# The forget gate's low-rank product on the unsplit residual, with the norm's column factors in its weights

## The chip, the cores and the metric

The kernel runs on one core of one Trainium2 chip. The metric is the time of one execution on the device, in microseconds (us). The engines are named as in the profile: PE multiplies matrices, PEld is its weight loads, DVE and ACT work elementwise, POOL does a few odd jobs and issues some DMAs, SP issues the other DMAs.

## The reference

One layer of a streaming encoder: 512 positions, model width 1024, all in float32.

```python
h = h + 0.5 * swiglu(rmsnorm(h, ffn1_norm), ffn1_w_in, ffn1_w_out)
z = rmsnorm(h, mix_norm) @ w_in
conv_a, conv_gt, q, k, v, r, g_lr = split(z)       # g_lr: 16 columns
y_conv = conv_module(conv_a, conv_gt, ...)          # GLU, causal depthwise conv of width 31, LayerNorm, silu
log_a = log_sigmoid(g_lr @ gate_w_up + gate_b) / 16 # forget gate, through rank 16
y_gla = gla(q, k, v, r, log_a)                      # chunked gated linear attention
h = h + concat([y_conv, y_gla]) @ w_out
h = h + 0.5 * swiglu(rmsnorm(h, ffn2_norm), ...)
h = h + sigmoid(rmsnorm(h, ple_norm) @ ple_w_gate) * (p @ ple_w_proj)
out = rmsnorm(h, final_norm)
```

`rmsnorm(h, g)` is `h * rsqrt(mean(h*h) + eps) * g`: a factor for each row (position) and a factor `g` for each column. The product that this case is about is `g_lr`, 1024 to 16.

## The kernel before, in words

Activations lie transposed: a tile holds 128 columns of the model (partitions) by 512 positions, so the residual is eight tiles `hT[0..7]`. Float32 products are made from fast ones: each operand is split into a high and a low part, and three products (high by high, high by low, low by high) are added in PSUM (`mm3`). For the mixer the residual is first multiplied by `mix_norm`'s column factors and then split; these eight pairs are `hg`. The row factor is not in them: it is multiplied in behind each product, by DVE, with the tile `bc` (`rsb` in the code), which holds the row factors spread over all partitions.

The engines' orders are the order of the code: `Ordered` chains the instructions of PE, DVE and ACT in the order in which they are written. POOL's order is left to the scheduler. Matmuls and nearly all else are recorded at L46, in that helper; what is told apart is told by tiles.

The place of the change is the start of the mixer, behind the first feed-forward part. PE makes, one after the other, with `zblock` (24 matmuls of 128x512: eight column tiles, three products each), the convolution's gate and value columns in blocks of 128: `pb0`, `pa0`, `pb1`, `pa1`, and later two more pairs. Two short steps are put between the matmuls of a `zblock`, through its argument `mid`: in `pa0` the column sums of squares (`colsum`), from which DVE and POOL make the row factors (`rsqrt_mean`: DVE `ms`, POOL `rs`, four small DVE instructions); in `pb1` the four transposes that spread them (`spread`), behind which ACT copies the result to `bc`. From then on DVE multiplies `bc` into `pb0` (tile `g`, then ACT's sigmoid, tile `s`) and `pa0` (`u`), makes the gated value (`glu_out`), and fills its time with the convolution's taps (`taps(n)`: n instructions of 482 to 511 positions each, tile `cv`).

The low-rank product stood behind `pa1`: its weights `gw` (128 x 8 x 32, both 16 columns and padding) were multiplied with `hg` as plain float32, in four 32-column strips of the array that sum every fourth column tile, once for the high and once for the low parts. That is 16 matmuls of 32x512; a plain float32 matmul stands in the trace as two records. DVE multiplied the result with `bc` (tile `glr`, named `glu` in the trace, since it shares a buffer with it), and PE's next product but one, with `gwu`, read it. `gw` is loaded by SP (L1036).

PSUM is eight banks; `bank()` hands them out in turn. At the end of the mixer PE waits in places on DVE and ACT: DVE finishes the taps, `y` times `r` is made for the attention's output, PE transposes it, and the LayerNorm of the convolution runs through DVE, ACT and PE.

Of the kernel before, what the change touches and what calls it, by code (L numbers as in the profile page):

```python
# [8 lines left out]
F32 = mybir.dt.float32  # L9
# [3 lines left out]
ALU = mybir.AluOpType  # L13
PSUM = bass.MemoryType.PSUM

P = 128
SEQ = 512
D = 1024
DC = D // P
# [8 lines left out]
TB = SEQ // P  # L28
RANK = 16
# [33 lines left out]
def block_kernel(ctx: ExitStack, tc: tile.TileContext, a: dict, out: bass.AP):  # L63
    nc = tc.nc
    pe, dve, act, pool = (Ordered(tc, e) for e in (nc.tensor, nc.vector, nc.scalar, nc.gpsimd))
# [15 lines left out]
    def nm(s):  # L81
        uid[0] += 1
        return f"{s}_{uid[0]}"
# [6 lines left out]
    def bt2(dt=F32R, s="a"):  # L90
        t = big.tile([P, 2, SEQ], dt, tag="A", bufs=NA, name=nm(s))
        hi, lo = t[:, 0], t[:, 1]
        whole_of[id(hi)] = hi, t
        return hi, lo

    def bt(dt=F32, s="a"):
        if dt not in other:
            t, other[dt] = bt2(dt, s)
            return t
        return other.pop(dt)  # L100
# [4 lines left out]
    def tmp(s, w=SEQ, dt=F32, bufs=2):  # L105
        return tp.tile([P, w], dt, tag=s, bufs=bufs, name=nm(s))
# [14 lines left out]
    def psum(pool_, n, shape, tag="mm"):  # L121
        return pool_.tile(shape, F32, tag=tag, bufs=n, name=nm("pd" if len(shape) == 3 else "ps"))

    def singles():
        return region("fixed", "spare" if mode[0] == 0 else stack[1][0] if len(stack) > 1 else "double", "singles")

    def bank():
        if mode[0] == 0:
            turn_no[0] += 1
            at = turn_no[0] % 7  # L130
            if at in (3, 4):
                return fixed()
            if at in (5, 6):
                return spare()
        return psum(singles(), 3, [P, SEQ])

    def fixed():
        return psum(region("fixed"), 2, [P, SEQ])

    def spare():  # L140
        return psum(region("fixed", "spare"), 2, [P, SEQ])
# [10 lines left out]
    def aux():  # L152
        if mode[0] == 2:
            return fixed()
        return psum(singles(), 1, [P, SEQ], "aux")
# [14 lines left out]
    col = cp.tile([P, ncol + 4 * WIDTH], F32, name="col")  # L170
    nc.scalar.dma_start(out=col, in_=a["columns"])
    cw = col[:, ncol:ncol + 4 * WIDTH]
    first_of, at = {}, 0
# [1 line left out]
        first_of[name] = at  # L175
        at += n

    def vec(name, c):
        at = first_of[name] + c
        return col[:, at:at + 1]  # L180

    warm = cp.tile([P, 1], F32, name="warm")
    act.copy(warm, ones)
# [39 lines left out]
    def high(r3):  # L223

        nk, nc_ = r3.shape[1], r3.shape[2]
        hi = wp.tile([P, 1024], F32R, tag="wh", bufs=6, name=nm("wh"))
        lo = wp.tile([P, 1024], F32R, tag="wl", bufs=6, name=nm("wl"))
        h3 = hi[:, :nk * nc_].rearrange("p (k c) -> p k c", k=nk)
        l3 = lo[:, :nk * nc_].rearrange("p (k c) -> p k c", k=nk)
        act.copy(h3, r3)  # L230
        return h3, l3, r3
# [17 lines left out]
    def mm3(ps, wh, wl, xh, xl, first, last):  # L249
        pe.matmul(ps, wh, xh, start=first, stop=False)  # L250
        pe.matmul(ps, wh, xl, start=False, stop=False)
        pe.matmul(ps, wl, xh, start=False, stop=last)
# [15 lines left out]
    def rows_of(w, k):  # L268

        part, kk = (w[k // 4], k % 4) if isinstance(w, list) else (w, k)  # L270
        return part[0][:, kk, :], part[1][:, kk, :]

    def zblock(w, x, mid={}):

        ps = bank()
        for k in range(DC):
            if k in mid:
                mid[k]()
            wh, wl = rows_of(w, k)
            mm3(ps, wh, wl, *x[k], k == 0, k == DC - 1)  # L280
        return ps

    def rsqrt_mean(ss, n, w, bufs=3, between=None):

        ms = tmp("ms", 16)[:, :w]
        dve.tensor_scalar(ms, ss, 1.0 / n, EPS, ALU.mult, ALU.add)
        r = tmp("rs0", 16)[:, :w]
        pool.tensor_tensor(out=r, in0=ms, in1=negh[:, :w], op=ALU.pow)
        if between is not None:
            between()  # L290
        t = tmp("rs1", 16)[:, :w]
        dve.tensor_tensor(out=t, in0=r, in1=r, op=ALU.mult)
        dve.tensor_tensor(out=t, in0=t, in1=ms, op=ALU.mult)
        dve.tensor_scalar(t, t, -0.5, 1.5, ALU.mult, ALU.add)
        rs = tmp(f"rs{bufs}", 16, bufs=bufs)[:, :w]
        dve.tensor_tensor(out=rs, in0=r, in1=t, op=ALU.mult)
        return rs

    def spread(col, copy=True):

        ps = aux()
        for j in range(TB):
            pe.transpose(ps[:, j * P:(j + 1) * P], col[:, j:j + 1].to_broadcast([P, P]), ident)
        if not copy:
            return ps
        bc = tmp("bc", bufs=1)
        act.copy(bc, ps)
        return bc

    def colsum(srcs):  # L310

        ps = aux()
        n = 0
        for s in srcs:
            for j in range(TB):
                pe.matmul(ps[:, n * TB + j:n * TB + j + 1], s[:, j * P:(j + 1) * P], ones,
                          start=True, stop=True)
            n += 1
        if n == 1:
            return ps[:, 0:TB]  # L320
        t = tmp("cs", 16)[:, :TB]
        dve.tensor_reduce(out=t, in_=ps[:, :n * TB].rearrange("p (n j) -> p j n", j=TB),
                          axis=mybir.AxisListType.X, op=ALU.add)
        return t
# [172 lines left out]
    hT = [big.tile([P, SEQ], F32, tag="H", bufs=DC, name=nm("h")) for _ in range(DC)]  # L497
    hg = []
# [49 lines left out]
    norm, mid = Norm(), []  # L548
# [400 lines left out]
    def sums_hooks(x, names, at):  # L949

        h = {}
        for name, key in zip(names, at):
# [14 lines left out]
    hg, norm = ffn(ffn1_in, a["ffn1_w_out"][0], xb, "mix_norm", {0: Left(ffn1_in, 0), 1: w1, 2: w2},  # L967
                   (ps0[:2], ps0[2:]), lambda: spread(mid[0]), hooks, (1,), FAR, CASTS, ADDS)
# [15 lines left out]
    def conv_steps(c):  # L984
        y, g, tap = acc[c], glu[c], cw[:, c * WIDTH:(c + 1) * WIDTH]
        dve.tensor_scalar(y, g, tap[:, PAD:WIDTH], vec("conv_b", c), ALU.mult, ALU.add)
        yield
        for w in range(PAD):
            late = PAD - w
            dve.scalar_tensor_tensor(out=y[:, late:], in0=g[:, 0:SEQ - late], scalar=tap[:, w:w + 1],  # L990
                                     in1=y[:, late:], op0=ALU.mult, op1=ALU.add)
            yield
# [22 lines left out]
    def glu_value(ps):  # L1015
        a1 = tmp("u1")
        dve.tensor_tensor(out=a1, in0=ps, in1=rsb, op=ALU.mult)
        return a1

    def glu_out(a1, sg):  # L1020
        g = bt(s="glu")
        dve.tensor_tensor(out=g, in0=a1, in1=sg, op=ALU.mult)
        glu.append(g)
        conv.append(conv_steps(len(glu) - 1))


    wb, wa = w_ahead
# [5 lines left out]
    mid = []  # L1033
    pb0 = zblock(wb[0], hg)
    gw = bt(s="gw")[:, 0:2 * DC * RANK].rearrange("p (k c) -> p k c", k=DC)
    nc.sync.dma_start(out=gw, in_=a["gate_down"])  # L1036
    w2a.append(high(raw_a[1]))
    raw_q = pair(C_Q)
    low(w2a[0])
    pa0 = zblock(wa[0], hg, {1: lambda: mid.append(rsqrt_mean(colsum([norm.acc]), D, TB))})  # L1040
    low(w2a[1])
    pb1 = zblock(wb[1], hg, {1: lambda: mid.append(spread(mid[0]))})
    rs, rsb = mid
    rs2 = tmp("rs2", 16, bufs=1)[:, :TB]
    dve.tensor_tensor(out=rs2, in0=rs, in1=rs, op=ALU.mult)
    raw_k = pair(C_K)
    sg = glu_gate(pb0)
    v = glu_value(pa0)
    glu_out(v, sg)
    wq = [added(high(raw_q[0]))]  # L1050
    taps(3)
# [4 lines left out]

    ps = bank()
    for k0 in range(0, DC, 4):  # L1060
        for i in range(2):
            for j in range(4):
                pe.matmul(ps[2 * RANK * j:2 * RANK * (j + 1)], gw[:, k0 + j, :], hg[k0 + j][i].bitcast(F32),
                          start=(k0 == i == 0), stop=(k0 + i == 5), skip_group_check=True)
    glr = bt(s="glr")
    taps(1)
    dve.tensor_tensor(out=glr, in0=ps, in1=rsb, op=ALU.mult)
    wq.append(added(high(raw_q[1])))


# [7 lines left out]
    for j in range(2):  # L1078
        ps = bank()
# [79 lines left out]
    k0 = zblock(wk[0], hg)  # L1159
# [115 lines left out]
    for t in range(TB):  # L1275
        ps = tokblock(wv, t, {5: lambda: chunk_sums(range(6)),
                             8: lambda: wr.append(high(raw_r[2])),
                             14: lambda: wr.append(high(raw_r[3]))} if t == 3 else {})
# [57 lines left out]
    for t in range(TB):  # L1336
        if t == 0:
            taps(3)
            ps = tokblock(wr, t, {5: lambda: chunk_sums([6]), 12: lambda: outputs(0)})
            chain(range(4, 7))  # L1340
            oload(4)
        elif t == 1:
            ps = tokblock(wr, t, {2: lambda: outputs(1)})
# [7 lines left out]
                                     in1=rs.unsqueeze(2).to_broadcast([P, TB, 4]), op0=ALU.mult, op1=ALU.mult)  # L1351
        else:
            ps = tokblock(wr, t)
# [90 lines left out]
    norm = Norm()  # L1444
# [25 lines left out]
    for k in range(4):  # L1470
        for n in range(3):
            w, ps = half[n]
# [22 lines left out]
    hg = nhg  # L1495
# [17 lines left out]
    mid = []  # L1513
# [97 lines left out]
    hg, norm = ffn(ffn2_in, a["ffn2_w_out"][0], xb, "ple_norm", wf, ((g0, u0), (g1_, u1_)), mid[1], hooks, (), {("m5", 1): 4, ("m6", 2): 3, ("m1", 3): 3, ("m2", 3): 3}, {("m6", 2): 4, ("m1", 3): 4})  # L1611
# [299 lines left out]
```

## Time and profile before

| | us |
|---|---|
| median of 3 runs | 930.98 (929.45 to 931.45) |
| the profiled execution | 929.6 |
| its span, first to last instruction | 927.9 |
| PE busy | 918.3 (99%) |
| DVE busy | 823.0 (89%) |
| ACT busy | 507.8 (55%) |
| granted TensorE clock, mean | 0.998 |

The profiled execution took 1.7 us more than its span, and 1.4 us less than the median. Start times are counted from the first instruction. PE's rows overlap: a matmul's record is longer than the distance to the next one's start, so that the cost of a matmul in a row of many is read from starts, not from durations.

### The profile page before, as it was taken

The page shows a single profiled execution, that of the slowest core. Times are in us where ns is not written, and L with a number is a line of the kernel's source. Part 1 is how long each engine was busy: PE and PEld are TensorE (multiplying, and loading weights), DVE is VectorE, ACT ScalarE, POOL GpSimd, SP SyncE. Part 2 cuts the span into 40 slices and gives each one's busy share as a digit, 9 for nine tenths or more (in the row PEclk, how much of TensorE's full clock was granted, in tenths as well). Part 3 has the DMA queues.
Part 4 walks back from the last instruction along what each step waited for, and adds up shares of the span by engine and source line. Part 5 has one row for each costly group of instructions (what it writes and reads, how often), then busy time and mean ns, then how long its engine had stood idle before and what let it go on. Part 6 is the DMA issues. An engine that isn't in the chain of part 4 may idle for free.

```text
span 927.9 us, 12878 instructions
## 1 busy us (share of the span) xinstructions
PE 918.3 (99%) x4982; PEld 782.4 (84%) x4982; DVE 823.0 (89%) x1098; ACT 507.8 (55%) x740; POOL 58.3 (6%) x73
## 2 busy tenths in 40 slices
PE   9999999999999999999999999999999999999996
PEld 8898888888888888788877889888888888888885
DVE  6699989999999876999986789899999999997896
ACT  7664355445444574463564875355445444456883
POOL 0120000000000111001120020000000000000120
PEclk9999999999999999999999999999999999999999
DMA  9433334224322693356552563334224322348463
GB/s 325 116 91 120 108 115 128 88 80 133 118 91 65 155 260 93 74 130 138 137 137 75 153 141 109 114 114 125 87 85 130 120 91 78 110 136 244 91 113 115
DMA packets 104175, 114.44 MB, mean 123 GB/s; under 512 B 3889, under 2 KB 90289, under 8 KB 104113
## 3 DMA queue, kind: packets, MB, share of 16 engines
q1 hardware_dynamic: 97664, 94.65, 32.8%
q0 software_dynamic: 6304, 18.88, 11.2%
q8 instruction: 39, 0.64, 0.3%
q14 instruction: 24, 0.19, 0.1%
q10 hardware_dynamic: 144, 0.09, 0.0%
HBM read 93.67 MB, written 2.10 MB: 103 GB/s over the span
## 4 chain that ended last, share of the span: by engine, by line
PE 99%; DVE 1%; issue 0%; ACT 0%; POOLq 0%; DVEq 0%
PE ps L46 59%; PE pd L46 40%; DVE u L46 0%; DVE rs L46 0%; ACT yc L46 0%; DVE y L46 0%; DVE g L46 0%; DVE s L46 0%; DVE yc L46 0%; POOLq L1907 0%; DVE ms L46 0%; DVE zeros L46 0%; DVE sse L46 0%; DVEq L46 0%; POOLq L46 0%
## 5 line engine op out<-in xcount | busy, mean ns | idle before, releaser
L46 DVE TENSOR_TENSOR wl<-wr,wh 128x1024 fp32r<-128x1024 f32 (+2 forms) x161 | 188.3, 1180 | 16.3 <-ACT wh L46 16.1
L46 ACT CAST wh<-wr 128x1024 fp32r<-128x1024 f32 (+2 forms) x178 | 176.2, 1021 | 20.7 <-PE ps L46 6.4
L46 PE MATMUL pd<-hg,wh 128*128 128x512 f32 x576 | 150.0, 391 | 0.0
L46 PE MATMUL ps<-act,wh 128*128 128x512 f32 x448 | 138.3, 390 | 0.0
L46 PEld LDWEIGHTS pd<-hg,wh 128*128 128x128 f32 x576 | 105.9, 188 | 21.0 <-DVE u L46 0.4
L46 PE MATMUL ps<-hg,wh 128*128 128x512 f32 (+1 forms) x448 | 117.3, 346 | 0.0
L46 PE MATMUL pd<-t,wh 128*128 128x512 f32 x392 | 98.2, 392 | 0.0
L46 PEld LDWEIGHTS ps<-act,wh 128*128 128x128 f32 x448 | 83.1, 188 | 16.5
L46 ACT ACTIVATE s<-g 128x512 f32<-128x512 f32 x48 | 30.4, 633 | 117.9 <-DVE g L46 117.9
L46 ACT COPY sq<-pd 128x1024 f32<-128x1024 f32 x45 | 45.7, 1016 | 87.3 <-PE pd L46 52.9
L46 PEld LDWEIGHTS ps<-hg,wh 128*128 128x128 f32 x448 | 78.0, 190 | 11.3 <-issue 1.3
L46 PE MATMUL ps<-act,wl 128*128 128x512 f32 x224 | 87.1, 389 | 0.0
L46 PE MATMUL pd<-hg,wl 128*128 128x256 f32 (+1 forms) x544 | 83.9, 289 | 0.0
L46 PEld LDWEIGHTS pd<-hg,wl 128*128 128x128 f32 x544 | 75.9, 190 | 6.3
L46 PEld LDWEIGHTS pd<-t,wh 128*128 128x128 f32 x392 | 70.5, 189 | 12.6
L46 PE MATMUL ps<-hg,wl 128*128 128x512 f32 (+1 forms) x224 | 77.1, 344 | 0.0
L46 ACT CAST wh<-sm 128x1024 fp32r<-128x1024 f32 x42 | 44.0, 1051 | 54.7 <-DVE sm L46 50.5
L46 PEld LDWEIGHTS pd<-t,wl 128*128 128x128 f32 x392 | 53.5, 190 | 3.8
L46 DVE TENSOR_TENSOR wl<-sm,wh 128x1024 fp32r<-128x1024 f32 x42 | 50.9, 1219 | 4.9 <-ACT wh L46 4.9
L46 DVE TENSOR_TENSOR sq<-pd,sq 128x1024 f32<-128x1024 f32 x45 | 54.8, 1218 | 0.4 <-PE pd L46 0.4
L46 PE MATMUL ps<-wh,hg 128*128 128x512 f32 x176 | 54.8, 392 | 0.0
L46 PE MATMUL pd<-t,wl 128*128 128x256 f32 x392 | 54.7, 282 | 0.0
(307 smaller groups left out, 1636.9 us busy)
## 6 DMA issues: line engine op xcount, KB each, us to landing
wr<-in_ffn_w_in SPq DMA_DIRECT2D x84, 512.0 KB, 3.7
wr<-in_ffn_w_out SPq DMA_DIRECT2D x32, 512.0 KB, 3.5
wr<-in_w_in SPq DMA_DIRECT2D x20, 512.0 KB, 5.1
wl<-wr POOLq DMA_DIRECT2D x18, 512.0 KB, 5.3
wr<-in_ffn_w_out SPq DMA_DIRECT2D x16, 384.0 KB, 3.1
wr<-in_w_out SPq DMA_DIRECT2D x8, 512.0 KB, 4.0
wq<-in_ple_w_gate SPq DMA_DIRECT2D x8, 512.0 KB, 3.8
wl<-wq POOLq DMA_DIRECT2D x8, 512.0 KB, 4.9
```

The lines of the kernel that those rows point to most:

```text
L46: inst = call(*args, **kwargs)
```

## The change

The low-rank product is made once, from the unsplit residual `hT`, instead of twice from the parts of `hg`. The column factors of `mix_norm`, which `hg` contains and `hT` does not, are multiplied into the weights `gw` by one DVE instruction (`gains`), put into `rsqrt_mean` between POOL's instruction and the four small ones of DVE. The eight matmuls stand directly behind the transposes of `spread`, inside `pb1`; the product with `bc` stands behind `pa0`'s, ahead of the first gated value.

```diff
@@ -175,9 +175,9 @@
         first_of[name] = at
         at += n
 
-    def vec(name, c):
+    def vec(name, c, n=1):
         at = first_of[name] + c
-        return col[:, at:at + 1]
+        return col[:, at:at + n]
 
     warm = cp.tile([P, 1], F32, name="warm")
     act.copy(warm, ones)
@@ -1034,18 +1034,35 @@
     pb0 = zblock(wb[0], hg)
     gw = bt(s="gw")[:, 0:2 * DC * RANK].rearrange("p (k c) -> p k c", k=DC)
     nc.sync.dma_start(out=gw, in_=a["gate_down"])
+    low_rank = []
+
+    def gains():
+        dve.tensor_tensor(out=gw, in0=gw, in1=vec("mix_norm", 0, DC).unsqueeze(2).to_broadcast([P, DC, 2 * RANK]),
+                          op=ALU.mult)
+
+    def spread_and_low_rank():
+        mid.append(spread(mid[0]))
+        ps = bank()
+        for k0 in range(0, DC, 4):
+            for j in range(4):
+                pe.matmul(ps[2 * RANK * j:2 * RANK * (j + 1)], gw[:, k0 + j, :], hT[k0 + j],
+                          start=(k0 == 0), stop=(k0 == 4), skip_group_check=True)
+        low_rank.append(ps)
+
     w2a.append(high(raw_a[1]))
     raw_q = pair(C_Q)
     low(w2a[0])
-    pa0 = zblock(wa[0], hg, {1: lambda: mid.append(rsqrt_mean(colsum([norm.acc]), D, TB))})
+    pa0 = zblock(wa[0], hg, {1: lambda: mid.append(rsqrt_mean(colsum([norm.acc]), D, TB, between=gains))})
     low(w2a[1])
-    pb1 = zblock(wb[1], hg, {1: lambda: mid.append(spread(mid[0]))})
+    pb1 = zblock(wb[1], hg, {1: spread_and_low_rank})
     rs, rsb = mid
     rs2 = tmp("rs2", 16, bufs=1)[:, :TB]
     dve.tensor_tensor(out=rs2, in0=rs, in1=rs, op=ALU.mult)
     raw_k = pair(C_K)
     sg = glu_gate(pb0)
     v = glu_value(pa0)
+    glr = bt(s="glr")
+    dve.tensor_tensor(out=glr, in0=low_rank[0], in1=rsb, op=ALU.mult)
     glu_out(v, sg)
     wq = [added(high(raw_q[0]))]
     taps(3)
@@ -1056,15 +1073,7 @@
 
 
 
-    ps = bank()
-    for k0 in range(0, DC, 4):
-        for i in range(2):
-            for j in range(4):
-                pe.matmul(ps[2 * RANK * j:2 * RANK * (j + 1)], gw[:, k0 + j, :], hg[k0 + j][i].bitcast(F32),
-                          start=(k0 == i == 0), stop=(k0 + i == 5), skip_group_check=True)
-    glr = bt(s="glr")
     taps(1)
-    dve.tensor_tensor(out=glr, in0=ps, in1=rsb, op=ALU.mult)
     wq.append(added(high(raw_q[1])))
 
 
```

On PE, at `pb1` (`ps_3309` before, `ps_3310` in the change) and the four transposes of the row factors (`ident`), `gw` are the low-rank weights, `hg` the split and `h` the unsplit residual. Before:

```order
L46 MATMUL ps_3309<-hg_3066,wa_2943 128x512 x3
L46 MATMUL ps_3313<-ident,rs_580_3285 128x128 x4
L46 MATMUL ps_3309<-hg_3078,wa_2943 128x512 x3
...
L46 MATMUL ps_3366<-hg_3192,wa_3046 128x512 x3
L46 MATMUL ps_3402<-hg_3066,gw_3258 32x512
...
L46 MATMUL ps_3402<-hg_3192,gw_3258 32x512
L46 MATMUL ps_3426<-hg_3066,wh_3214 128x512 x2
```

In the change, at the same place:

```order
L46 MATMUL ps_3310<-hg_3066,wa_2943 128x512 x3
L46 MATMUL ps_3314<-ident,rs_580_3286 128x128 x4
L46 MATMUL ps_3321<-h_104,gw_3258 32x512
...
L46 MATMUL ps_3321<-h_111,gw_3258 32x512
L46 MATMUL ps_3310<-hg_3078,wa_2943 128x512 x3
...
L46 MATMUL ps_3378<-hg_3192,wa_3046 128x512 x3
L46 MATMUL ps_3419<-hg_3066,wh_3214 128x512 x2
```

The 16 matmuls between `pa1` and the next block are gone, and eight stand between the transposes and the rest of `pb1`.

On DVE, from the row factors (`ms`, `rs`) to the first block's taps (`cv`). Before:

```order
L46 TENSOR_SCALAR ms_3277<-ps_3272 128x4
L46 TENSOR_TENSOR rs_579_3281<-rs_578_3279 128x4
...
L46 TENSOR_TENSOR g_587_3347<-ps_3233,bc_3318 128x512
L46 TENSOR_TENSOR u_589_3351<-ps_3268,bc_3318 128x512
L46 TENSOR_TENSOR gw_3258<-u_589_3351,s_3349 128x512
...
L46 TENSOR_TENSOR g_592_3362<-ps_3309,bc_3318 128x512
...
L46 TENSOR_TENSOR glu_3400<-ps_3402,bc_3318 128x512
L46 TENSOR_SCALAR cv_3203<-glu_3400,col 128x512
```

In the change:

```order
L46 TENSOR_SCALAR ms_3277<-ps_3272 128x4
L46 TENSOR_TENSOR gw_3258<-gw_3258,col 128x256
L46 TENSOR_TENSOR rs_579_3282<-rs_578_3279 128x4
...
L46 TENSOR_TENSOR g_588_3357<-ps_3233,bc_3319 128x512
L46 TENSOR_TENSOR u_590_3361<-ps_3268,bc_3319 128x512
L46 TENSOR_TENSOR gw_3258<-ps_3321,bc_3319 128x512
L46 TENSOR_TENSOR glu_3364<-u_590_3361,s_3359 128x512
...
L46 TENSOR_TENSOR g_594_3374<-ps_3310,bc_3319 128x512
```

The weights' factor is new between `ms` and `rs`; the low-rank result's product (named `glu` before and `gw` now, for the buffer it shares) stands two rows behind `g` instead of at the end of the second block's taps. POOL's two instructions that set the tile `keep` come ahead of two DMAs instead of behind them.

## The prediction

> **What bounds the kernel now.** First the page: busy shares and the chain that ended last.
>
> ```profile
> PE 918.3 (99%) x4982; PEld 782.4 (84%) x4982; DVE 823.0 (89%) x1098; ACT 507.8 (55%) x740; POOL 58.3 (6%) x73
> PE 99%; DVE 1%; issue 0%; ACT 0%; POOLq 0%; DVEq 0%
> ```
>
> PE is both the busiest engine and nearly the whole chain. A time taken off PE should therefore come off the end, as long as nobody else sets PE's starts. So next PE's waits (in total, times, longest), and the stretches of the mixer (PE, PEld, DVE, ACT, POOL busy, then clock, DMA share and GB/s).
>
> ```profile
> PE ps L46 <- DVE zeros L46: 1.1, 1, 1.1
> PE ps L46 <- ACT yc L46: 0.2, 1, 0.2
> ```
>
> ```profile
> 375.00:400.00 25.00, 25.00 (x108) 19.99 (x107) 24.70 (x40) 11.61 (x15) 0.86 (x1) 1.00 0.28 73
> ...
> 425.00:450.00 25.00, 25.00 (x277) 20.04 (x276) 24.76 (x45) 11.05 (x19) 0.52 (x1) 1.00 0.36 94
> ...
> 462.00:477.00 15.00, 15.00 (x74) 12.61 (x73) 12.19 (x25) 10.24 (x27) 6.92 (x5) 1.00 0.41 98
> ```
>
> PE waits for no DMA, and but once behind the start. But DVE has nothing to spare at 375 to 400 and 425 to 450 (24.70 and 24.76 of 25), and first has some at 462 to 477 (12.19 of 15): whether it can follow a PE that comes earlier is the real question. The granted clock is 1.00 in these stretches.
>
> **What the low-rank product costs.** PE's starts around it, and one stretch of plain matmuls for the pitch; below, the weight loads of its groups.
>
> ```profile
> 347.74 6.28 PE L46 MATMUL ps<-hg,wa 128*128 128x512 f32 x27
> 353.87 0.95 PE L46 MATMUL ps<-ones,xg 128*128 128x1 f32 x8
> ...
> 370.02 1.07 PE L46 MATMUL ps<-hg,wa 128*128 128x512 f32 x4
> 371.01 3.64 PE L46 MATMUL ps<-hg,gw 128*32 128x512 f32 x32
> 374.59 0.73 PE L46 MATMUL ps<-hg,wh 128*128 128x512 f32 x2
> 375.16 0.39 PE L46 MATMUL ps<-hg,wl 128*128 128x512 f32 x1
> ```
>
> ```profile
> 371.47 0.13 PEld L46 LDWEIGHTS ps<-hg,gw 128*32 128x32 f32 x4 [0.30 <-issue]
> ...
> 373.62 0.13 PEld L46 LDWEIGHTS ps<-hg,gw 128*32 128x32 f32 x4 [0.30 <-issue]
> ```
>
> Pitch of a plain matmul: (353.87 - 347.74)/27 = 0.227. The last of `pa1` starts at 370.02 + 3 x 0.227 = 370.70; the third of the next block starts at 375.16 and would start at 370.70 + 3 x 0.227 = 371.38 without the product. It costs 3.78. Inside, 32 records run as eight groups of four that start together (four strips of the array), six of their loads stand at even distances from 371.47 to 373.62, (373.62 - 371.47)/5 = 0.43 a group: eight make 3.44, and 0.34 is the change from and to the full array (0.09 in: 371.01 instead of 370.93; the rest out).
>
> **The change, term by term.** *Removed:* 16 matmuls, 3.78 on PE. *Added:* eight matmuls, 16 records, four groups: 4 x 0.43 = 1.72, plus the way in and out. The operands are float32 as before, so I take the same group time. The way in is now from the transposes:
>
> ```profile
> 360.26 0.60 PE L46 MATMUL ps<-ident,rs 128*128 128x128 f32 x4
> 360.61 10.47 PE L46 MATMUL ps<-hg,wa 128*128 128x512 f32 x45
> ...
> 452.02 0.39 PE L46 MATMUL ps<-v,sc 128*128 128x128 f32 x2
> 452.33 1.09 PE L46 MATMUL ps<-st,q 64*64 64x128 f32 x24
> ```
>
> The trace has no step from transposes to strips. The nearest row is 452.02: two 128x128 matmuls on the full array, then quarter arrays. The four transposes show a pitch of (360.61 - 360.26)/4 = 0.09 to 0.11; at 452 two matmuls take 0.31, so the step costs about 0.09 there, as at 371.01. Bounds: if the transposes' own break in the stream already pays for the step, the new product costs 1.72 and the change saves 2.06. If the four groups did not overlap at all, each would take its record's 0.61,
>
> ```profile
> 373.62 0.61 PE L46 MATMUL ps<-hg,gw 128*32 128x512 f32 x4
> ```
>
> together 2.44 + 0.34 = 2.78, and 1.00 is saved. I take the value of the nearest rows: 1.72 + 0.34 = 2.06, saved 3.78 - 2.06 = **1.72**.
>
> On that step the Trainium skill has a rule ("TensorEngine Tiling (Array Packing)", section "Tiling Modes"): changing the tiling mode drains TensorE. By it there are two changes of mode before and two after, none is saved, and the sum stays 1.72; without a drain of its own it would be 2.06. The trace agrees with the rule: about 0.09 extra into strips at 371.01 and into quarters at 452.33.
>
> *The weights' factor on DVE* is one 128x256 product, 0.42 by the nearest row. It stands where DVE waits for POOL:
>
> ```profile
> L46 DVE TENSOR_TENSOR n<-h 128x256 f32<-128x256 f32 x2 | 0.8, 416 | 0.0
> ```
>
> ```profile
> 27.89 0.16 DVE L46 TENSOR_SCALAR ms<-ps 128x4 f32<-128x4 f32 x1 [5.76 <-PE ps L46]
> 30.12 0.16 DVE L46 TENSOR_TENSOR rs<-rs 128x4 f32<-128x4 f32 x1 [0.92 <-POOL rs L46]
> ...
> 354.85 0.16 DVE L46 TENSOR_SCALAR ms<-ps 128x4 f32<-128x4 f32 x1 [1.37 <-PE ps L46]
> 356.18 0.16 DVE L46 TENSOR_TENSOR rs<-rs 128x4 f32<-128x4 f32 x1 [1.17 <-POOL rs L46]
> 356.78 0.16 DVE L46 TENSOR_TENSOR rs<-rs,rs 128x4 f32<-128x4 f32 x1
> ```
>
> The gap of 1.17 takes it. At 27.89, with DVE at work beside POOL, `ms` to `rs` took 2.23 instead of 1.33, so up to 0.9 may be added; still `rs` is done by 357.9 and the transposes start at 360.26. Cost zero, cover 2.4. The factor waits for `gw`'s DMA: issued at 346.9, landed 5.4 later,
>
> ```profile
> L1036 SPq DMA_DIRECT2D gw<-in_gate_down x1: 459/459/459, 346.9 to 346.9; - x1
> DMA to landing us min/median/max: 5.4/5.4/5.4
> ```
>
> at 352.3, 2.6 before its place; behind it wait only the row factors with their 2.4.
>
> *What is pushed on DVE.* `pb1` now ends 2.06 later, since the low-rank product stands inside it. DVE's rows there:
>
> ```profile
> 363.45 0.69 DVE L46 TENSOR_TENSOR gw<-u,s 128x512 f32<-128x512 f32 x1 [0.66 <-ACT s L46]
> ...
> 366.16 0.68 DVE L46 TENSOR_TENSOR g<-ps,bc 128x512 f32<-128x512 f32 x1
> ...
> 374.72 0.69 DVE L46 TENSOR_TENSOR glu<-ps,bc 128x512 f32<-128x512 f32 x1 [0.64 <-PE ps L46]
> 375.33 0.54 DVE L46 TENSOR_SCALAR cv<-glu,col 128x512 f32<-128x512 f32 x1
> ```
>
> The low-rank result's product moves from 374.72 into the 0.66 in front of 363.45, where DVE waited for the sigmoid: free. `pb1`'s product `g` (366.16) must now wait: `pb1`'s 21 remaining matmuls ended at 360.61 + 0.11 + 20 x 0.227 + 0.39 = 365.65, now at 367.71, so `g` comes 1.6 later, and with it the sigmoid, and on ACT behind it a weight cast, its DMA on POOL and SP's next load; no PE wait names a DMA, so that lateness is covered. Up to 375.33 DVE gets back the wait of 0.64 and the 0.61 of the moved product: it is 0.3 later than before. PE meanwhile is 1.72 earlier. The two meet at the end of the mixer:
>
> ```profile
> 473.84 0.74 DVE L46 SCALAR_TENSOR_TENSOR cv<-glu,col,cv 128x502 f32<-128x502 f32 x1
> 476.52 0.69 DVE L46 TENSOR_TENSOR y<-y,r 128x512 f32<-128x512 f32 x1 [1.94 <-ACT r L46]
> ...
> 477.78 0.60 PE L46 MATMUL ps<-ident,y 128*128 128x128 f32 x4
> ...
> 488.85 1.02 PE L46 MATMUL ps<-p,mean 128*128 128x512 f32 x2
> ```
>
> Here DVE, done at 474.58, waited 1.94 for `r`, which ACT makes of PE's product. With the change `r` is there at 474.80 and DVE at 474.9: nearly all of its reserve is used, but not more. `y` ends at 475.6, PE's transposes could start at 477.78 - 1.72 = 476.06. About 0.45 is left. Behind this point DVE and ACT wait for PE in a ring (the last taps and the LayerNorm's sums reach PE at 488.85, all counted from these transposes), so everything comes 1.72 earlier, to the end.
>
> POOL's setting of `keep` moves ahead of two weight DMAs; POOL stands idle 9.47 before the first, so it costs nothing.
>
> ```profile
> 365.62 0.92 POOL L46 DMA_DIRECT2D wl<-wr  x1 [9.47 <-ACT wl L46]
> ```
>
> **Sum.** Profiled execution: 929.6 - 1.72 = 927.9, span 926.2. The median of the runs stands 1.4 above that execution; against it, 930.98 - 1.72 = **929.26**. What a measurement of this kernel can tell from no change is about 0.2%, 1.86 us: the forecast lies just inside.
>
> **The rivals.** *The step is free* (saved 2.06): 928.9. For it: the transposes already interrupt the stream. Against: the row at 452.33. *DVE eats the gain*: the reserve at 476.52 is spent to within 0.45. If DVE arrives more than 0.8 later than before instead of 0.3, PE's transposes wait, and from 2.5 on nothing is saved: 929.3 to 931.0. For it: DVE's 99% in the stretches before; against: in between DVE also waited for ACT and POOL, which may shrink:
>
> ```profile
> DVE r L46 <- ACT r L46: 0.5, 1, 0.5
> DVE rs L46 <- POOL rs L46: 0.2, 1, 0.2
> ```
>
> *The groups don't run side by side* in the new place, the other side: the eight matmuls as 16 records one after the other, 16 x 0.43 + 0.34 = 7.2, that is 3.4 more than before, 934.4; slower than before from 0.215 a record. Against it: the same four strips, four loads in 0.13 in every group.
>
> **How the numbers follow.** The forecast 62%, the free step 15%, DVE 15%, no overlap 3%, and 5% for what I don't see. The three runs lie 2.0 apart, so a median is good to about 0.5. The forecast (0.14 inside the bound) then reads faster 25, same 37; the free step faster 11, same 4; DVE faster 2, same 12, slower 1; no overlap slower 3; the rest 2, 2, 1. Faster 0.40, same 0.55, slower 0.05. The range takes in the free step less the scatter of a median, and at the top no gain: 928.1 to 931.1.
>
> **What would show it.** Right: 16 records of 128*32 directly behind the transposes at 360.3, about 2 long; `g` of `pb1` waits 1.2 to 1.6 for PE; `y`'s wait for `r` near zero; PE's matmuls of 488.85 at 487.1; span 926.2. Wrong: a new PE wait for DVE at the transposes of `y` or at 488.85; `rs` reaching PE late at 360; records of the new product that start one by one.

## The result, and the profile after

Seven runs of each on one chip: the change 927.82 us (927.41 to 928.45), the kernel before 930.38 (929.45 to 931.45). The ratio is 0.9972, 95% interval 0.9963 to 0.9981: faster by 0.28%. The profiled execution took 927.76, its span is 926.0, and the mean granted clock 0.997 (0.998 before). The prediction was 929.26 with a range from 928.1, so the time is 1.4 less than predicted and 0.3 below the range.

The page's first line of the change:

```profile
PE 916.4 (99%) x4966; PEld 782.1 (84%) x4966; DVE 823.0 (89%) x1099; ACT 507.7 (55%) x740; POOL 58.4 (6%) x73
```

PE is busy 1.9 less, with 16 records fewer. Its waits behind the start are the one line of before, for ACT's `yc`: no new wait has come. PE's starts in the change, from the column sums to the block behind `pa1`, and then at the end of the mixer (start, us from the first start to the last end, what, count):

```profile
353.76 1.05 PE L46 MATMUL ps<-ones,xg 128*128 128x1 f32 x8
...
360.22 0.60 PE L46 MATMUL ps<-ident,rs 128*128 128x128 f32 x4
360.75 1.92 PE L46 MATMUL ps<-h,gw 128*32 128x512 f32 x16
362.60 10.49 PE L46 MATMUL ps<-hg,wa 128*128 128x512 f32 x45
372.93 0.62 PE L46 MATMUL ps<-hg,wh 128*128 128x512 f32 x2
373.38 0.39 PE L46 MATMUL ps<-hg,wl 128*128 128x512 f32 x1
...
475.99 0.60 PE L46 MATMUL ps<-ident,y 128*128 128x128 f32 x4
...
487.03 1.02 PE L46 MATMUL ps<-p,mean 128*128 128x512 f32 x2
```

The 16 records stand behind the transposes. From the transposes to the next plain matmul it is 2.38 where it was 0.35, so the product costs 2.03 there. The third matmul behind `pa1` starts at 373.38 instead of 375.16: 1.78 earlier, of which 0.04 is there at the transposes of the row factors already (360.22 instead of 360.26). The transposes of `y` come 1.79 earlier, the LayerNorm's sums 1.82. The loads of the four groups, in the change:

```profile
360.75 0.16 PEld L46 LDWEIGHTS ps<-h,gw 128*32 128x32 f32 x8 [0.17 <-issue]
361.20 0.13 PEld L46 LDWEIGHTS ps<-h,gw 128*32 128x32 f32 x4 [0.30 <-issue]
361.63 0.13 PEld L46 LDWEIGHTS ps<-h,gw 128*32 128x32 f32 x4 [0.30 <-issue]
```

The first row holds two groups' loads, the others one each, 0.43 to 0.45 apart: the strips run side by side as before. DVE in the change, from the weights' factor to the mixer's end:

```profile
354.92 0.41 DVE L46 TENSOR_TENSOR gw<-gw,col 128x256 f32<-128x256 f32 x1
356.28 0.16 DVE L46 TENSOR_TENSOR rs<-rs 128x4 f32<-128x4 f32 x1 [0.94 <-POOL rs L46]
...
362.74 0.69 DVE L46 TENSOR_TENSOR gw<-ps,bc 128x512 f32<-128x512 f32 x1
363.42 0.69 DVE L46 TENSOR_TENSOR glu<-u,s 128x512 f32<-128x512 f32 x1
...
367.69 0.69 DVE L46 TENSOR_TENSOR g<-ps,bc 128x512 f32<-128x512 f32 x1 [1.49 <-PE ps L46]
...
375.54 0.54 DVE L46 TENSOR_SCALAR cv<-glu,col 128x512 f32<-128x512 f32 x1
...
473.45 0.73 DVE L46 SCALAR_TENSOR_TENSOR cv<-glu,col,cv 128x502 f32<-128x502 f32 x1
474.74 0.69 DVE L46 TENSOR_TENSOR y<-y,r 128x512 f32<-128x512 f32 x1 [0.55 <-ACT r L46]
```

The factor (0.41) lies in the wait for POOL, which still ends in a wait of 0.94. The result's product stands where the 0.66 of waiting was. `g` of `pb1` waits 1.49 for PE. DVE is 0.21 late at 375.54 and has 0.55 of its reserve of 1.94 left at `y`.

So the two profiled executions differ by little more than what was summed (1.72): by 1.84 in time and 1.9 in span, of which 0.11 is there at the column sums, ahead of the change (353.76 instead of 353.87). What the sum does not hold is the rest of the difference between the medians: 930.98 stood as the level of before, and the profiled executions lie at 929.6 and 927.76.

### The profile page after: what moved, and what is told of

Read it like the earlier page. It is cut to its first block, busy times and chain, and to the rows that moved or that the text cites. A ratio compares the mean times of both kernels' runs of the same rounds, so it can differ in the third digit from the quotient of the medians.

```text
span 926.0 us, 12846 instructions
## 1 busy us (share of the span) xinstructions
PE 916.4 (99%) x4966; PEld 782.1 (84%) x4966; DVE 823.0 (89%) x1099; ACT 507.7 (55%) x740; POOL 58.4 (6%) x73
## 3 DMA queue, kind: packets, MB, share of 16 engines
q0 software_dynamic: 6304, 18.88, 11.3%
## 4 chain that ended last, share of the span: by engine, by line
PE 99%; DVE 1%; issue 0%; ACT 0%; POOLq 0%; DVEq 0%
PE ps L46 59%; PE pd L46 40%; DVE u L46 0%; DVE rs L46 0%; ACT yc L46 0%; DVE y L46 0%; DVE g L46 0%; DVE s L46 0%; DVE yc L46 0%; POOLq L1916 0%; DVE ms L46 0%; DVE zeros L46 0%; DVE sse L46 0%; DVEq L46 0%; POOLq L46 0%
## 5 line engine op out<-in xcount | busy, mean ns | idle before, releaser
L46 DVE SCALAR_TENSOR_TENSOR cv<-glu,col,cv 128x502 f32<-128x502 f32 (+24 forms) x90 | 63.2, 730 | 0.6
```

Of the source, the lines that this page charges most:

```text
L46: inst = call(*args, **kwargs)
```

## Experiments

Two theories on that rest were put up at first. S: it is scatter, and only the counted steps are real. X: a usual execution of before holds time that its profiled one did not show, and that the change loses. The first four experiments repeat both kernels and take the change apart.

**The kernel before again, and the change again (no edit).**

> The kernel before, unchanged, against itself. The traces of before and of the change differ by 1.9 us of span, their medians by 2.6. Theory S (scatter): nothing but the counted steps changed, and the other 0.7 is the scatter of the runs of before (929.45 to 931.45); this run then has a ratio of 1.000, and its medians may differ by up to 0.5 us from the other set of runs of the same kernel. Theory X (something more): the usual execution of before holds some 0.7 us that its one profiled execution (929.6, among the fastest) did not show; then this run lies near 930.4 again, and its own profile, if it is of a usual execution, has a span near 928.7 and shows where.

> The change, unchanged, timed again beside e1. S: 1.8 us faster than before (ratio 0.998), as its trace shows step by step (PE 1.77 earlier at 373, 1.83 at 501, 1.85 at the end). X: 2.5 us faster again (ratio 0.9973).

Measured: before 930.62 (929.37 to 932.05, 11 runs), ratio 1.0002 (0.9993 to 1.0010); the change 928.31 (927.63 to 929.25, 10 runs), ratio 0.9978 (0.9969 to 0.9987). The profile of this repetition is of an execution of 932.05, 2.45 more than the profiled one of before, with the same program. That makes the time that came and went visible. First a load of `w_in` by SP, the last of five in a row, ACT at the cast that reads it, and PE at the column sums (already shown for before: 353.87) in the kernel before as first profiled:

```profile
L216 SPq DMA_DIRECT2D wr<-in_w_in x1: 1974/1974/1974, 328.8 to 328.8; - x1
DMA to landing us min/median/max: 10.7/10.7/10.7
...
339.54 1.05 ACT L46 CAST wh<-wr 128x1024 fp32r<-128x1024 f32 x1 [1.30 <-PE pd L46]
```

The same in the repetition, and PE's first matmuls of `pb0`:

```profile
L216 SPq DMA_DIRECT2D wr<-in_w_in x1: 1996/1996/1996, 329.3 to 329.3; - x1
  ACT wh L46: 3.1, 1
DMA to landing us min/median/max: 12.9/12.9/12.9
...
342.28 1.05 ACT L46 CAST wh<-wr 128x1024 fp32r<-128x1024 f32 x1 [3.14 <-DMA wr<-in_w_in]
...
349.09 4.77 PE L46 MATMUL ps<-hg,wa 128*128 128x512 f32 x19 [1.00 <-ACT hg L46]
```

And in the change, as first profiled:

```profile
L216 SPq DMA_DIRECT2D wr<-in_w_in x1: 1650/1650/1650, 329.0 to 329.0; - x1
DMA to landing us min/median/max: 7.6/7.6/7.6
...
338.13 1.04 ACT L46 CAST wh<-wr 128x1024 fp32r<-128x1024 f32 x1
```

The load lands 7.6 to 12.9 after its issue. The cast is for a weight that is needed much later, but ACT works in the order written, and the casts that make `hg` stand behind it; so PE, which reads `hg`, starts `pb0` late. In before, 1.30 of waiting is put down to PE, but the load landed at 328.77 + 10.67 = 339.44, 0.1 before the cast's start. In a later trace (rows swapped in the change) it landed at 339.47, and a wait of 1.31 at the same cast is put down to the load. So it was most likely the load in before too, where PE's first matmul of `pb0` came at 347.74 without a wait. This is X's place; whether the change is free of it was still open.

**Half the product at the old place.** The low-rank product from `hT` with the factor in the weights, but behind `pa1`:

```diff
     def spread_and_low_rank():
         mid.append(spread(mid[0]))
-        ps = bank()
-        for k0 in range(0, DC, 4):
...
-        low_rank.append(ps)
...
-    dve.tensor_tensor(out=glr, in0=low_rank[0], in1=rsb, op=ALU.mult)
...
     glu_out(glu_value(pa1), sg)
+    ps = bank()
+    for k0 in range(0, DC, 4):
...
     taps(1)
+    dve.tensor_tensor(out=glr, in0=ps, in1=rsb, op=ALU.mult)
```

> The halving alone: column factors in the weights, unsplit residual, eight matmuls, but behind pa1 where the product stood. S: 4 groups of 0.43 fewer, 1.72 us faster (about 928.7 against 930.4, ratio 0.9982), DVE's wait of 0.64 for the product goes to zero and pb1's gate does not wait. X: 1.7 if the additional gain comes with the place, 2.5 if it comes with the smaller product.

**Only moved.** All 16 matmuls from `hg`, without the factor, behind the transposes:

```diff
     def spread_and_low_rank():
         mid.append(spread(mid[0]))
         ps = bank()
         for k0 in range(0, DC, 4):
-            for j in range(4):
-                pe.matmul(ps[2 * RANK * j:2 * RANK * (j + 1)], gw[:, k0 + j, :], hT[k0 + j],
-                          start=(k0 == 0), stop=(k0 == 4), skip_group_check=True)
+            for i in range(2):
+                for j in range(4):
+                    pe.matmul(ps[2 * RANK * j:2 * RANK * (j + 1)], gw[:, k0 + j, :], hg[k0 + j][i].bitcast(F32),
+                              start=(k0 == i == 0), stop=(k0 + i == 5), skip_group_check=True)
```

> The move alone: all 16 matmuls with the split residual, behind the transposes inside pb1, no factor in the weights. S: the product costs the same 3.8 us in either place, less perhaps 0.05 at the step from the transposes: time within 0.1 of before. DVE's gate of pb1 comes 3.2 later, the low-rank product's result is also late, DVE is some 2 us behind at the end of the mixer, where it had 1.94: about even. If DVE eats more than that, 0.3 slower. X: 0.7 faster if the additional gain comes with the place.

Measured: half at the old place 929.02 (927.75 to 930.75, 11 runs), ratio 0.9986 (0.9977 to 0.9995); only moved 930.67 (929.02 to 932.79, 12 runs), ratio 1.0002 (0.9994 to 1.0011). PE in the trace of the first:

```profile
372.38 1.92 PE L46 MATMUL ps<-h,gw 128*32 128x512 f32 x16
...
374.82 0.40 PE L46 MATMUL ps<-hg,wl 128*128 128x512 f32 x1
```

and of the second:

```profile
362.43 0.60 PE L46 MATMUL ps<-ident,rs 128*128 128x128 f32 x4
362.95 3.64 PE L46 MATMUL ps<-hg,gw 128*32 128x512 f32 x32
366.52 10.54 PE L46 MATMUL ps<-hg,wa 128*128 128x512 f32 x45
```

From the first record of the product to the same matmul behind it: 374.82 - 372.38 = 2.44, before 375.16 - 371.01 = 4.15, so halving is worth 1.71. The move: 366.52 - 362.43 - 0.35 = 3.74 in the new place, 3.78 in the old. The move by itself gives at most 0.04. In time the halving alone is faster, the move alone can't be told from no change; neither time says more, since the start of the mixer was late in both traces (PE's column sums at 355.16 and 355.94).

**ACT's weight casts behind those of `hg`.** In the kernel before and in the change, the chain of ACT runs on from the feed-forward part, so that four casts of weights can no longer come between `hg`'s; DVE's low parts of them go where it waits for the transposes, and in the change `gw`'s load goes ahead of these weights' loads:

```diff
-    in_order(True)
+    pe.last = dve.last = None
...
-    low(w2b[0])
-    low(w2b[1])
...
-    low(w2a[0])
...
+    low(w2b[0])
+    low(w2b[1])
+    low(w2a[0])
     low(w2a[1])
```

> The kernel before, with ACT's four casts of the later gate and value weights put behind the casts of hg (and DVE's low parts of them behind the row factors), so that hg waits for no weight load. X (the usual execution of before holds some 0.7 us at the start of the mixer because ACT waits there for a w_in load that lands between 7 and 13 us after its issue): the wait cannot occur, the executions lie within 1.5 us of each other, median 929.0 to 929.7, 0.7 to 1.4 less than before. S (the executions scatter by chance, this place is not the reason): median 930.2 to 930.6 as before, spread 2.5 to 3.5. A loss of up to 0.5 is possible in both if DVE, with four low parts of 1.22 in its gap of 3.36, reaches the end of the mixer later.

> The changed kernel with the same casts put behind hg's, and the load of gw ahead of these weights' loads. X: median 1.75 below the previous kernel (the terms of the sum alone, since the scatter of the load is out of both), 927.2 to 927.9, spread under 1.5; as fast as the change or up to 0.7 faster. S: as the change, 927.8 to 928.3, and 2.3 below the previous kernel.

Measured: before with it 929.78 (929.04 to 930.42, 11 runs), ratio 0.9994 (0.9986 to 1.0003); the change with it 928.50 (927.82 to 929.08, 11 runs), ratio 0.9977 (0.9969 to 0.9986). The scatter shrinks as X says: 1.4 and 1.3 wide, where 27 runs of before beside them are 3.1 wide (928.92 to 931.99); standard deviations 0.43 and 0.40 against 0.80. The load itself was no earlier (10.7 again in the first), it only found nobody waiting. That fits X, but the width of some ten runs proves little by itself: the kernel with DVE later (below) keeps the wait, and its ten runs have a standard deviation of 0.43 too. The table of all traces below is the better evidence. Both medians missed their bands. In before the casts behind give about 0.6 (930.35 - 929.78), a little under the 0.7 expected, and the interval of the ratio still holds no change; the difference of the two kernels' means is 1.28, not 1.75 (from the standard deviations good to 0.35). In the second's trace PE is 0.32 earlier than in the change's first one up to 865 and loses that at 869, where it waits 0.2 for DVE's `h`, after a wait of 0.46 at DVE for ACT that the change's trace does not have. What makes this wait is open.

**The change a third time (no edit), and two kernels with neighbouring rows swapped.** With 17 runs the change had shown a scatter of only 1.84, as if it were free of the late load, though nothing ahead of the mixer differs. P: it is; C: that was chance. The swaps leave all ahead of the mixer as it is:

```diff
-    glr = bt(s="glr")
-    dve.tensor_tensor(out=glr, in0=low_rank[0], in1=rsb, op=ALU.mult)
     glu_out(v, sg)
+    glr = bt(s="glr")
+    dve.tensor_tensor(out=glr, in0=low_rank[0], in1=rsb, op=ALU.mult)
```

in the change, and in the kernel before

```diff
-    taps(1)
     dve.tensor_tensor(out=glr, in0=ps, in1=rsb, op=ALU.mult)
+    taps(1)
```

> The changed kernel once more, for its scatter: 17 runs of it so far lie within 1.84 us (standard deviation about 0.5), 79 of the kernel before within 3.3 (about 0.85). P (in the change the load of w_in lands in time, for a reason of the program): again within 1.9, median 927.8 to 928.3, none above 929.4. C (it is by chance): spread 2.5 to 3.3, median 928.3 to 928.8, some runs above 929.5.

> The change with the low-rank result's product one row later on DVE, behind the first gated value instead of in front of it. Nothing ahead of the mixer differs. DVE is 0.6 later from 363.5 up to the wait of g for pb1 (1.49 long), which takes it in: no time is lost, within 0.3 of the change. If the gap of 0.66 in front of the gated value was what made the product free, 0.1 to 0.6 is lost at the end of the mixer. For the scatter, P: as the change, within 1.9; C: 2.5 to 3.3.

> The kernel before with two neighbouring rows of DVE swapped at 374.7 (the low-rank result's product ahead of a tap): it waits 0.6 longer for PE there, and the reserve of 1.94 takes it in. No time is lost or won: 930.2 to 930.6, scatter as before, 2.5 to 3.3. A scatter under 1.9 would say that the lateness of the load hangs on the program and not on what it computes.

Measured: the change 928.36 (927.42 to 929.89, 11 runs), ratio 0.9984 (0.9975 to 0.9992); swapped in the change 928.18 (927.34 to 930.61), 0.9985 (0.9976 to 0.9994); swapped in before 931.27 (929.32 to 932.28), 1.0007 (0.9998 to 1.0016). C holds, with a spread of 2.47 in the change, just under its 2.5, and of 3.27 in the change with rows swapped: the change scatters like before, and its third profile shows it with the load late:

```profile
L216 SPq DMA_DIRECT2D wr<-in_w_in x1: 1651/1651/1651, 329.0 to 329.0; - x1
  ACT wh L46: 3.1, 1
DMA to landing us min/median/max: 12.5/12.5/12.5
...
341.66 1.05 ACT L46 CAST wh<-wr 128x1024 fp32r<-128x1024 f32 x1 [3.13 <-DMA wr<-in_w_in]
...
348.46 4.78 PE L46 MATMUL ps<-hg,wa 128*128 128x512 f32 x19 [0.61 <-DVE h L46]
...
353.53 2.14 PE L46 MATMUL ps<-hg,wa 128*128 128x512 f32 x8 [0.28 <-DVE hg L46]
```

Of the rows swapped in the change, DVE:

```profile
363.33 0.69 DVE L46 TENSOR_TENSOR gw<-u,s 128x512 f32<-128x512 f32 x1 [0.66 <-ACT s L46]
363.94 0.69 DVE L46 TENSOR_TENSOR glr<-ps,bc 128x512 f32<-128x512 f32 x1
...
367.60 0.69 DVE L46 TENSOR_TENSOR g<-ps,bc 128x512 f32<-128x512 f32 x1 [1.01 <-PE ps L46]
```

The product no longer uses the 0.66, and `g`'s wait shrinks from 1.49 to 1.01 instead: the same cover, one step later. Nothing is lost (927.75 in the profiled execution, 927.76 in the change). The swap in before lost nothing in its trace either, since PE's lateness is there ahead of the swap (1.5 at the column sums) and grows by only 0.1 behind; its median lies above the band, in the profiled execution the load took 12.5; whether that holds for the other runs, one trace can't say.

**The product three column tiles later.** It then starts from plain matmuls and not from the transposes:

```diff
-    pb1 = zblock(wb[1], hg, {1: spread_and_low_rank})
+    pb1 = zblock(wb[1], hg, {1: lambda: mid.append(spread(mid[0])), 4: low_rank_part})
```

> The change with the low-rank product nine matmuls further on in pb1, so that it starts from a plain matmul of the full array and not from the transposes. By the forecast (the way in costs 0.09 in both places) its distance between the matmuls around it exceeds the pitch by 2.06, as directly behind the transposes. If the transposes' break had paid for the way in, it costs 0.1 to 0.3 more here than behind them. The result's product on DVE waits 1.5 to 2 for PE, ahead of a wait of 1.5 that shrinks by the same, so the time stays within 0.5 of the change.

One execution, 928.33. PE in its trace:

```profile
360.60 0.60 PE L46 MATMUL ps<-ident,rs 128*128 128x128 f32 x4
360.95 2.31 PE L46 MATMUL ps<-hg,wa 128*128 128x512 f32 x9
363.19 1.93 PE L46 MATMUL ps<-h,gw 128*32 128x512 f32 x16
365.05 2.14 PE L46 MATMUL ps<-hg,wa 128*128 128x512 f32 x8
```

365.05 - 360.95 - 9 x 0.227 = 2.06, against 2.03 behind the transposes. Both figures hold the way in and the way out; from the product's first record to the next plain matmul it is 1.86 here and 1.85 there, so the way in costs the same in both places to within 0.03. The product's wait on DVE was 2.05, at the upper end of the 1.5 to 2 expected, and `g` behind it then did not wait.

**DVE later by 2.4.** Four products whose results nobody uses, in the change behind the second gated value:

```diff
     glu_out(glu_value(pa1), sg)
+    for _ in range(4):
+        dve.tensor_tensor(out=tmp("u1"), in0=rsb, in1=rsb, op=ALU.mult)
```

> The change with four more DVE products of 128x512 (about 0.61 each, 2.4 in all, results unused) behind the second gated value. If DVE's reserve at the end of the mixer is what the prediction says (0.55 of wait at y in the change's profile, and about 0.45 before PE's transposes of y): y waits no longer for r, PE's transposes come 1.4 to 1.9 later than in the change, median 929.4 to 929.9. If DVE has more room elsewhere (the waits for ACT and POOL in between shrink): under 0.5 is lost, 928.0 to 928.5. If DVE was already at its limit: 2.4, 930.4.

Measured: 930.67 (929.97 to 931.53, 10 runs), ratio 1.0001 (0.9992 to 1.0010), by the median nearest to the third answer. PE in its trace:

```profile
424.58 0.51 PE L46 MATMUL ps<-wl,hg 128*128 128x512 f32 x1 [0.88 <-DVE wl L46]
...
478.61 0.66 PE L46 MATMUL ps<-ident,y 128*128 128x128 f32 x4 [0.32 <-DVE y L46]
```

PE was 0.74 late ahead of this (a load landed after 11.3). At 424.58 it loses 1.1 to a low part of a weight that DVE makes, a place that the expectation had not named, and 0.7 more before the transposes of `y`; behind the column sums the kernel is 2.1 longer than the change (table below), so only some 0.3 of the 2.4 is hidden. The wait at `y`, 0.55 in the change, did not take it in. First ACT's row ahead of `r` in the change, then the same row, `r` and `y` in this trace:

```profile
467.18 1.14 ACT L46 ACTIVATE r<-ps,rs 128x128 f32<-128x128 f32 x4 [1.27 <-DVE rs L46]
```

```profile
470.37 1.14 ACT L46 ACTIVATE r<-ps,rs 128x128 f32<-128x128 f32 x4 [2.49 <-DVE rs L46]
...
477.02 0.81 ACT L46 ACTIVATE r<-ps,rs 128x512 f32<-128x512 f32 x1
...
477.87 0.69 DVE L46 TENSOR_TENSOR y<-y,r 128x512 f32<-128x512 f32 x1 [0.49 <-ACT r L46]
```

`y` still waits 0.49 for `r`, because `r` is 3.0 later itself (477.02 instead of 474.02). ACT waits for DVE's tile `rs` at 470.37, and from there to `r` it has no wait. In the kernel before it did not wait there at all. So a later DVE makes `r` later too, and the wait at `y` is no reserve against it.

**All traces on one scale.** When the load landed, where PE's column sums start, and the span less that start:

| kernel | landed | sums start | span | rest |
|---|---|---|---|---|
| before, first profile | 339.44 | 353.87 | 927.9 | 574.0 |
| before again | 342.18 | 356.21 | 930.3 | 574.1 |
| rows swapped in before | 341.36 | 355.38 | 929.5 | 574.1 |
| only moved | 341.92 | 355.94 | 930.1 | 574.2 |
| before, casts behind | 339.41 | 353.65 | 927.7 | 574.1 |
| the change, first profile | 336.65 | 353.76 | 926.0 | 572.2 |
| the change again | 336.45 | 354.12 | 926.5 | 572.4 |
| the change, third time | 341.56 | 355.59 | 928.0 | 572.4 |
| rows swapped in the change | 339.47 | 353.75 | 926.0 | 572.3 |
| half at the old place | 337.49 | 355.16 | 927.6 | 572.4 |
| three tiles later | 338.98 | 354.11 | 926.6 | 572.5 |
| the change, casts behind | 336.67 | 353.51 | 926.1 | 572.6 |
| the change, DVE later | 340.47 | 354.50 | 928.9 | 574.4 |

Three things can be read off. The rest is 574.0 to 574.2 in the five traces without the halving, whatever the load does, and 572.2 to 572.4 in the four of the change and its swap: by the means, 574.09 and 572.32, the change is worth 1.77. And from a landing at 340.5 on, the sums start 14.03 behind it, in all five such traces (14.02 to 14.03): there each microsecond of the load is one of the kernel.

Third, another load does the same, the first of the five. ACT waits for it in every trace; here in the change's first profile and in half at the old place:

```profile
329.04 1.14 ACT L46 CAST wa<-wr 128x512 fp32r<-128x512 f32 x2 [1.28 <-DMA wr<-in_w_in]
```

```profile
330.44 1.14 ACT L46 CAST wa<-wr 128x512 fp32r<-128x512 f32 x2 [1.81 <-DMA wr<-in_w_in]
```

The column sums start 24.72 behind this cast in both (353.76 and 355.16), and just so in the change again (329.40 and 354.12) and in three tiles later (329.39 and 354.11). So the last load goes with the start of the mixer in five traces and the first one in four; in the other four, at 353.51 to 353.87, neither does. One of these four is the change with the casts behind: there the first cast stood at 329.64, which would give 354.36, and the sums started at 353.51, so this lateness was taken in too.

## Why the prediction was right and wrong

*The sum was right.* 1.72 was predicted; 1.78 stands in PE's starts behind `pa1`, 1.77 in the rest of the table, 1.71 for the halving by itself. The group's time of 0.43, four groups, the full way in and out: all as in the new rows. The one execution that could be set against its own profile came out as said, 927.76 for 927.9 and a span of 926.0 for 926.2. Some luck is in how close it came: in both of these executions the mixer started within 0.11 of the same time, where all 13 traces range over 2.7.

*The way in* was taken as 0.09 on the strength of one row; 2.03 behind the transposes and 2.06 behind plain matmuls show that the transposes' break pays for no more than 0.03 of it. The rival of the free step is out: in the trace PE gained 1.78, not 2.06, though the medians of the result, 2.56 apart, would by themselves speak for it. By the Trainium skill ("TensorEngine Tiling (Array Packing)", section "Tiling Modes") a change of the tiling mode drains TensorE; the traces agree, with 2.03 and 2.06 where four groups alone make 1.72.

*DVE* behaved as foretold up to 375 (0.21 late, 0.3 was said; `g` waited 1.49, 1.2 to 1.6 was said). By 473.45 it was 0.39 earlier than before, not 0.3 later, because a wait of 0.48 for ACT's `r` at 468.75 had fallen away; so 0.55 of waiting was left at `y` where about none had been expected. The prediction's reserve at 476.52 was a wrong reading all the same: "`r`, which ACT makes of PE's product" leaves out that ACT, on the way to `r`, also waits for DVE (1.27 at 467.18 in the change). The added work on DVE showed it, and showed a weight's low part at 424 that is limited earlier than `y`. For this change neither made a difference, PE waits for DVE in neither place.

*The factor, the load of `gw`, POOL's `keep`* cost nothing, as said.

*The step that failed is the level.* "The median of the runs stands 1.4 above that execution; against it, 930.98 - 1.72": the level of before was taken from three runs, and "a median is good to about 0.5" set the range. The median of all 106 runs of before (those beside each set, and its repetition) is 930.35, 0.63 lower. Medians of three, drawn from these 106 runs, have a standard deviation of 0.56, so that 0.5 was no bound. Of the 1.4 between the median and the profiled execution, then, 0.63 is how far the three runs lay above the level; 0.75 is what a usual execution takes longer than the profiled one, and the traces show its like at the start of the mixer, not behind it.

The 1.44 by which 929.26 was too high falls into four: 0.63, the level; 0.05, the term (1.77, not 1.72); 0.37, by which the change's 28 runs (median 928.21, 927.41 to 929.89) lie under 930.35 - 1.77; and 0.39, by which the seven runs of the result lie under these 28. The first and the last can be the chance of few runs: three runs have a median of 930.98 or more in 15 of 100 draws from the 106, seven a median of 927.82 or less in 8 of 100 from the 28. The third is not accounted for. By the means, 930.44 and 928.32, the difference is 2.12 with an interval of 0.30 to both sides, a little more than 1.77. Without the result's own runs it is 1.96 with 0.35, which holds 1.77, and the pair with the casts behind says 1.28 with 0.35, a little less. The chip makes little of it: on the three chips of the experiments, before had medians of 930.31, 930.35 and 930.17. The change over all its runs lies inside the range, at its lower end; the first result was below it. The 1.86 that was held for the least that can be told from no change was too much as well: the result's interval is 0.8 wide to each side.

What stays open is why the last load lands early or late. It is the last of three loads that SP issues within 2 us in before (327.0, 327.5 and 328.8), and four adding transfers of POOL follow from 330.8 on. In the four traces in which it took 7.1 to 7.7, it landed ahead of all four of these; in the nine others one to three of them landed first, though they were issued 1.7 us or more behind it. The two go together; that one makes the other is not shown, since no experiment took POOL's transfers or the other loads away. What was shown is the way from two landings to PE, and that the traces of one kernel differ ahead of the column sums and hardly behind them. No version here beats the change: with the casts put behind, its mean is 928.46, the change's 928.32; the former only has no late executions (at most 929.08, the change 929.89).

## What to carry to other kernels

A profiled execution that lies well under a median of three runs is itself a reading: either the few runs lie high, or the others hold time that it does not show. Here it was both, about half each. The forecast against the profiled execution came within 0.2, the one against the median missed by 1.4. Look for the hidden time where an engine that works in written order waits for a load and the chained work stands behind: here a landing only 0.1 ahead of its reader, put down to another engine, was the sign. A wait is a reserve only if what is waited for does not itself hang on the waiting engine. To tell a gain of 2 us from such a wait, compare spans counted from a point behind the wait, not whole times.

## What the runs showed of the hardware

The same load, at the same place of the program, took 7.1 to 12.9 us from issue to landing in 13 traces. The runs of the kernel before have a standard deviation of 0.8; its two traces differ by 2.4 in span and by 0.1 behind the column sums, and in all 13 traces these sums started 14.03 behind this load's landing whenever it landed at 340.5 or later.
